# Two-layer encoder in split fp32: the last wide layer's second product in three sweeps over raw tiles, its weight sums made in the second attention

## The chip, the cores and the metric

The kernel is one launch on one core of a Trainium2 chip; input and output lie in the device's memory. The number is the device time in microseconds (us). Engines are named as in the profile: PE is TensorE (PEld its weight load), DVE is VectorE, ACT ScalarE, POOL GpSimd, SP SyncE, which here only issues DMAs.

## The reference

512 tokens of width 1024 pass two layers. Each layer adds an attention and then an MLP to the residual `h`, each on an RMS-normalised `h`. Layer 0 has a grouped-query and a latent attention side by side; layer 1 ("the second attention", C) has 16 heads of 64 in which each query sees a window of 8 x 16 grid neighbours, with a learned bias. A final RMSNorm ends it.

```python
def sq_relu_mlp(h, w_up, w_down):            # 1024 -> 4096 -> 1024
    u = jax.nn.relu(h @ w_up)
    return (u * u) @ w_down

for layer in range(2):
    hn = rmsnorm(h, norm_mix[layer])
    h = h + (hybrid_attention(hn, ...) if layer % 2 == 0
             else neighbourhood_attention(hn, od_w_qkv[i], od_rpb[i], od_w_out[i]))
    h = h + sq_relu_mlp(rmsnorm(h, norm_ffn[layer]), ffn_w_up[layer], ffn_w_down[layer])
return rmsnorm(h, final_norm)
```

All is fp32. The change lies in the MLP of layer 1 and in the second attention.

## The kernel before

**Products.** An fp32 operand is split in two parts, `hi` (a copy rounded by ScalarE) and `lo` (the difference, on VectorE); a product is three matmuls, hi x hi, hi x lo, lo x hi. Activations stand transposed: tile k holds 128 rows of the width and 512 columns, the tokens. The residual is `hT`, 8 such tiles; the MLP's hidden layer is 32 tiles. A *plain* product uses matmuls of 512 tokens (L501 to L503).

**Seven products.** `Seven` computes a 2 x 2 block product with seven block products instead of eight: the blocks are two k tiles ("a pair", kp) by two column groups of 128 in the weight, and two halves of 256 tokens. A matmul is then 256 wide (L388 to L390). The scheme needs sums of weight blocks, made by GpSimd in `seven_chunk` (L302 to L304; 256 KB of weight each, split at L308 and L309), and sums of token blocks, made by `Seven.sums` (L336, L338, L340, normally on GpSimd) and split by `Seven.split` (L362, L363).

**Weights.** `weights(i)` hands out chunk i of one list in order of use. SP loads five chunks ahead, the split is made two chunks ahead, and the split weights have three buffers. A `Slot` is a 256 KB buffer of a pool of 30.

**The second attention** (`attend_C`, some 640 to 815 us) works in 32 half-heads. `rest(w, us, ripe)` is called once in each: it fills TensorE with pieces of the q, k, v projection (`fill.run`), finishes an older head and normalises two blocks of softmax rows (`norm`: a reciprocal on VectorE, L1429, a multiplication on GpSimd, L1430), which TensorE then transposes (L1452). The order of instructions is written out by hand here (`fixed_order`), each engine's own. GpSimd's queue also moves q and k blocks there (L1338, L1358, L1359); SP loads weights and the bias.

**The MLP of layer 1** is `mlp(1, last)` with the sizes (6, 8, 6, 8, 4):

| from, us | to, us | stage | form |
|---|---|---|---|
| 837 | 869 | first product, 6 hidden tiles | plain |
| 869 | 898 | second product of these 6 | plain |
| 898 | 937 | first product, 8 tiles | seven |
| 937 | 981 | second product of these 8 | plain |
| 981 | 1070 | first product, 18 tiles: 6 split, 8 kept raw (fp32), 4 split | seven |
| 1070 | 1109 | second product of the 6; beside it `convert` makes the token sums of the 8 raw tiles, on VectorE | plain |
| 1109 | 1151 | second product of the 8, four groups m of 256 columns | seven |
| 1151 | 1184 | second product of the last 4 (`down`, two column halves c), norm, output | plain |

`hT` is turned back to token-major by 4 x 4 x 2 transposes (`turn(i, c)`, L1615 to L1619): those of c = 0 stand beside the seven-product second product (m 2 and 3), those of c = 1 in `down`.

Of the kernel before, what the change touches and what calls it, by code (L numbers as in the profile page):

```python
# [35 lines left out]
def encoder_kernel(ctx: ExitStack, tc: tile.TileContext, ins, out, dbg=None):  # L36
# [242 lines left out]
    def catch_up():  # L279
        take_up(off_d)  # L280
        take_up(off_a)
# [491 lines left out]
    rope_q(0)  # L773


    kst = Slot()

    def ev_kr(b):
# [331 lines left out]
    def first_product(l):  # L1110
# [7 lines left out]
        xp = [s_.pair() for s_ in X]  # L1118
        U, R = [], []
        rb = keep([P, S], F32, "rb")  # L1120
        state = dict(c=SIZES[l][0], ids=None, plain=False, split=iter(()))
        x7 = Seven(KD)

        def ev(j, b):
# [62 lines left out]
        def ahead():  # L1187
            state["ids"] = x7.plan(w, P * state["c"])

        def stage(n, raw=0, more=0):  # L1190

            if not state["plain"]:
                plain()
            left = n + raw + more - len(U)
            while left:
                i = state["ids"]
                state["c"] += 2
                left -= 2
                if left:
                    ahead()  # L1200
                for _ in x7.run(i, raw_evac if more <= left < more + raw else pair_evac):
# [13 lines left out]
    def bias_rows():  # L1215
        R, Fi, Fe = Slot(F32), Slot(F32), Slot(F32)
        rpb = ins["od_rpb"][0]
        for qr in range(8):
            SP.dma_start(R.t[16 * qr : 16 * qr + 16, 0:248],
                           rpb.rearrange("h a b -> h (a b)")[:, (7 - qr) * 31 : (7 - qr) * 31 + 248])  # L1220
            yield
        POOL.memset(Fi.t[:, 0:376], NEG)
        POOL.memset(Fe.t[:, 256:512], NEG)
        rv = R.t[:, 0:248].rearrange("p (k d) -> p d k", d=31)
        POOL.tensor_copy(Fi.t[:, 0:376].rearrange("p (j k) -> p j k", k=8)[:, 15:31, :], rv[:, 7:23, :])
        POOL.tensor_copy(Fe.t[:, 0:248].rearrange("p (j k) -> p j k", k=8), rv)
# [12 lines left out]
        for s_ in (R, Fi, Fe):  # L1239
            s_.free()  # L1240
        yield

    def convert(u7, R):
        held = tc.keep_in_program_order
# [167 lines left out]
    def attend_C(step):  # L1412
# [138 lines left out]
    def step(n):  # L1551
# [3 lines left out]
        if n == 12:  # L1555
# [3 lines left out]
            for x in rest:  # L1559
                fill.add(*x)  # L1560

    fill.run(LEAD)
    with fixed_order():
        fixed[0] = 1
        attend_C(step)
        give_low(len(ready))
        fixed[0] = 0
    ok = [s_.pair() for s_ in O[5:]]
# [8 lines left out]
    def last_mlp():  # L1577
# [43 lines left out]
        def down(k0, c, up, tail):  # L1621
# [5 lines left out]
            def run():  # L1627
                banks = group(4)

                def use(k, j):  # L1630
                    wh, wl = (x[:, k % 2, :] for x in weights(ids[k // 2]))
                    uh, ul = (up[k][:, z, j * P : (j + 1) * P] for z in range(2))
                    PE.matmul(banks[j], uh, wh, start=k == 0, stop=False)
                    PE.matmul(banks[j], uh, wl, start=False, stop=False)
                    PE.matmul(banks[j], ul, wh, start=False, stop=k == nk - 1)

                for k in range(nk - tail):
                    for j in range(4):
                        use(k, j)
                for j in range(4):  # L1640
                    for k in range(nk - tail, nk):
                        use(k, j)
                    if c == 0:
                        turn(j, 1)
                    add(j, c, banks[j])
                    (first_half, last_half)[c](j)
                    if c == 0 and j == 3:

                        ACT.activation(tiny(1), ones[:, 0:1], AF.Sqrt)
# [5 lines left out]
        def last(k0, tiles_):  # L1655
# [4 lines left out]
            def beside(m, i):  # L1660
                if m == 2 and i == 0:
# [67 lines left out]
```

## Time and profile before

| | us |
|---|---|
| three runs | 1183.44, 1183.66, 1183.66 (median 1183.66) |
| the profiled execution, its own time (span) | 1184.0 |
| TensorE busy in it | 1160.5 |
| VectorE, ScalarE, GpSimd busy | 883.2, 640.3, 526.1 |

The profiled execution is 0.3 us from the median. A window's row gives, for a stretch of the span, the time in which each engine was busy and its instructions, then the granted TensorE clock (1.00 is full), the mean busy share of the 16 DMA engines and the GB/s that they moved. A matmul's own duration (0.28 or 0.40 us) overlaps the next one's, so the cost of a matmul is the distance between starts. A row of a line's group gives operation, operands, shape and count, then busy us and mean ns of one, then the engine's idle time before it and what ended it.

### The profile page before, as it was taken

Reading aid. Unit: us, or ns where it says so; the run is one execution under the profiler, and the core shown is the slowest. Engines: PE = TensorE matmul, PEld = TensorE weight load, DVE = VectorE, ACT = ScalarE, POOL = GpSimd, SP = SyncE. Lnnn points to the kernel's source line nnn. Section 1 sums busy time; section 2 is a strip of 40 time slices with the busy share of each in tenths; the row PEclk is TensorE's granted clock in tenths of the full one; section 3 lists DMA queues with packets and bytes.
Section 4 is the critical chain, followed back from the end, with each engine's and each line's share of the span. In section 5 each row is a group of like instructions: output and inputs, shape, how many; then the busy total and the mean of one; then the engine's idle time right before and its main releaser. Section 6 shows DMA issues by size and latency. Waiting matters only on the chain.

```text
span 1184.0 us, 19784 instructions
## 1 busy us (share of the span) xinstructions
PE 1160.5 (98%) x7128; PEld 1021.2 (86%) x7128; DVE 883.2 (75%) x1514; ACT 640.3 (54%) x1081; POOL 526.1 (44%) x662
## 2 busy tenths in 40 slices
PE   9989999999999999999999999999999999999997
PEld 8667778888899899988998998988889989998895
DVE  5788998878967368786884676667996736778975
ACT  4468676664546247562553565555554624666344
POOL 3267343224562377819602232231376625774710
PEclk9999999999999999999999999999999999999998
DMA  7223225212524723225226464433352341322412
GB/s 244 71 54 92 68 78 134 62 56 77 167 86 134 263 70 90 72 90 165 67 72 178 131 184 126 116 112 109 107 165 76 115 134 55 98 64 89 143 36 71
DMA packets 110145, 128.01 MB, mean 108 GB/s; under 512 B 9075, under 2 KB 86816, under 8 KB 110048
## 3 DMA queue, kind: packets, MB, share of 16 engines
q1 hardware_dynamic: 106992, 119.30, 33.5%
q0 software_dynamic: 2304, 6.31, 2.2%
q8 instruction: 56, 0.92, 0.3%
q10 hardware_dynamic: 752, 1.15, 0.3%
q14 instruction: 41, 0.34, 0.1%
HBM read 104.32 MB, written 6.29 MB: 93 GB/s over the span
## 4 chain that ended last, share of the span: by engine, by line
PE 81%; DVE 4%; ACT 1%; issue 1%; POOL 0%; DVEq 0%; ACTq 0%
PE mm L503 8%; PE mm L501 8%; PE mm L502 8%; PE mm L390 4%; PE mm L389 4%; PE mm L388 4%; PE t L388 3%; PE t L389 3%; PE t L390 3%; PE s L502 2%; PE s L503 2%; PE s L501 2%; PE s L390 2%; PE s L388 2%; PE s L389 2%; PE s L997 2%
## 5 line engine op out<-in xcount | busy, mean ns | idle before, releaser
L309 DVE TENSOR_TENSOR wlo<-a,whi 128x896 fp32r<-128x896 f32 x132 | 161.8, 1230 | 83.7 <-ACT whi L308 82.9
L308 ACT ACTIVATE whi<-a 128x896 fp32r<-128x896 f32 x132 | 125.0, 950 | 155.0 <-PE o L502 45.8
L501 PE MATMUL mm<-a,whi 128*128 128x512 f32 x485 | 195.9, 406 | 0.9 <-DVE a L915 0.7
L503 PE MATMUL mm<-a,wlo 128*128 128x512 f32 x485 | 192.1, 397 | 2.5 <-DVE wlo L202 2.5
L502 PE MATMUL mm<-a,whi 128*128 128x512 f32 x485 | 192.5, 397 | 0.1
L202 DVE TENSOR_TENSOR wlo<-raw,whi 128x1024 fp32r<-128x1024 f32 (+4 forms) x117 | 139.3, 1193 | 66.4 <-ACT whi L212 63.9
L212 ACT ACTIVATE whi<-raw 128x1024 fp32r<-128x1024 f32 (+3 forms) x120 | 116.4, 971 | 92.2 <-PE s L502 39.8
L302 POOL TENSOR_TENSOR a<-a 128x128 f32<-128x128 f32 x132 | 85.1, 645 | 173.3 <-DMA a<-in_ffn_w_up_dram 103.9
L303 POOL TENSOR_TENSOR a<-a 128x256 f32<-128x256 f32 x132 | 120.2, 910 | 10.3
L304 POOL TENSOR_TENSOR a<-a 128x128 f32<-128x128 f32 x132 | 115.1, 872 | 10.3
L503 PEld LDWEIGHTS mm<-a,wlo 128*128 128x128 f32 x485 | 91.7, 189 | 23.7 <-DVE wlo L202 3.4
L501 PEld LDWEIGHTS mm<-a,whi 128*128 128x128 f32 x485 | 91.8, 189 | 20.4 <-PE t L972 0.9
L502 PEld LDWEIGHTS mm<-a,whi 128*128 128x128 f32 x485 | 91.9, 190 | 17.4 <-DVE a L545 0.4
L388 PE MATMUL mm<-a,whi 128*128 128x256 f32 x370 | 103.9, 281 | 0.0
L389 PE MATMUL mm<-a,whi 128*128 128x256 f32 x370 | 103.9, 281 | 0.0
L390 PE MATMUL mm<-a,wlo 128*128 128x256 f32 x370 | 103.7, 280 | 0.0
L1005 POOL TENSOR_SCALAR p<-p,ti 128x512 f32<-128x512 f32 x64 | 46.2, 724 | 92.3 <-DVE ti L1004 81.1
L1430 POOL TENSOR_SCALAR p<-p,ti 128x256 f32<-128x256 f32 x64 | 35.6, 567 | 104.8 <-DVE ti L1429 91.8
L388 PE MATMUL t<-a,whi 128*128 128x256 f32 x264 | 74.2, 281 | 0.0
L389 PE MATMUL t<-a,whi 128*128 128x256 f32 x264 | 74.1, 281 | 0.0
L390 PE MATMUL t<-a,wlo 128*128 128x256 f32 x264 | 73.9, 280 | 0.0
L390 PEld LDWEIGHTS mm<-a,wlo 128*128 128x128 f32 x370 | 69.6, 188 | 0.2 <-DVE wlo L309 0.2
(338 smaller groups left out, 3210.8 us busy)
## 6 DMA issues: line engine op xcount, KB each, us to landing
a<-in_ffn_w_up_dram SPq DMA_DIRECT2D x104, 256.0 KB
raw<-in_ffn_w_down_dram SPq DMA_DIRECT2D x46, 512.0 KB
raw<-in_od_w_qkv_dram SPq DMA_DIRECT2D x64, 128.0 KB
a<-in_ffn_w_down_dram SPq DMA_DIRECT2D x28, 256.0 KB
raw<-in_ffn_w_up_dram SPq DMA_DIRECT2D x12, 512.0 KB
raw<-in_ev_w_in_dram SPq DMA_DIRECT2D x12, 384.0 KB
a<-a SPq DMA_DIRECT2D x18, 256.0 KB
bias<-bx SPq DMA_DIRECT2D x16, 256.0 KB
```

Of the source, the lines that this page charges most:

```text
L202: z = lambda: (eng or DVE).tensor_tensor(to, src, f32(high), op=ALU.subtract)
L212: ACT.activation(hi[:, 0:m], raw[:, 0:m], AF.Copy)
L303: POOL.tensor_tensor(r[:, 4:6], r[:, 2:3].to_broadcast([P, 2, P]), r[:, 0:7:6], op=ALU.add)
L304: POOL.tensor_tensor(r[:, 7], r[:, 3], r[:, 5], op=ALU.subtract)
L308: ACT.activation(hi[:, 0:896], raw[:, 128:1024], AF.Copy)
L309: DVE.tensor_tensor(lo[:, 0:896], raw[:, 128:1024], f32(hi[:, 0:896]), op=ALU.subtract)
L388: PE.matmul(o, wh, x[:, 0], start=kp == 0 and n in (0, 1, 3, 5), stop=False, skip_group_check=True)
L389: PE.matmul(o, wh, x[:, 1], start=False, stop=False, skip_group_check=True)
L390: PE.matmul(o, wl, x[:, 0], start=False, stop=kp == self.np - 1, skip_group_check=True)
L501: PE.matmul(o, wh, xh, start=first, stop=False)
L502: PE.matmul(o, wh, xl, start=False, stop=False)
L503: PE.matmul(o, wl, xh, start=False, stop=last)
```

## The change

Layer 0's MLP is the same work (its code now takes the first size from `FIRST`). Layer 1's MLP becomes `mlp_swept`: 6 plain tiles and their plain second product as before, then the first product of all other 26 tiles in one stretch (13 groups, 52 weight chunks, instead of 8 + 18 tiles with a plain product between); 22 of the tiles stay raw, the last 4 go to `down` as before. The second product of the 22 tiles (11 pairs) is a seven-product in another arrangement, `Sweeps`: the seven block products are dealt to three passes over all 11 pairs, two products in passes 0 and 1, three in pass 2, for all 1024 columns at a time, and each pass adds its banks straight into `hT`. `convert` and the plain second products of 8 and 6 tiles are gone.

The token blocks are made pair by pair by `tokens`, a step ahead: differences on GpSimd, splits on ScalarE and VectorE. The weight blocks are made by `SumsAhead` during the second attention, one step in each of `rest` 1 to 22: per pair four sums on GpSimd and two loads and two stores of 512 KB on GpSimd's queue, into a device buffer `made`. SP then loads the blocks from the weight (pass 0) or `made` (passes 1 and 2). The 16 transposes `turn(j, 0)` and their 4 copies move into `down` for c = 0, between its main part and its tail.

```diff
+    class SumsAhead:
+        def load(self, kp):
+            ...
+                for z, s_ in enumerate(self.raw[kp]):
+                    POOL.dma_start(s_.t, self.w[k * P : (k + 1) * P, :])
+        def steps(self):
+            self.load(0)
+            self.load(1)
+            yield
+            for kp in range(self.n):
+                ...
+                POOL.tensor_tensor(a22, a21, a22, op=ALU.add)
+                POOL.tensor_tensor(a21, a11, a21, op=ALU.subtract)
+                if kp:
+                    self.load(kp + 1)
+                yield
+                POOL.tensor_tensor(a11, a22, a11, op=ALU.subtract)
+                POOL.tensor_tensor(a12, a12, a11, op=ALU.subtract)
+                for z, s_ in enumerate(two):
+                    POOL.dma_start(self.made[kp, z], s_.t)
+                    s_.free()
+                yield
...
+    def sweep_chunk(w, k0, kind, made):
+        ...
+        if kind == 0:
+            for z in range(2):
+                SP.dma_start(line(a[:, S * z : S * z + S]), half(k0 + z, 0))
+        else:
+            for z in range(2):
+                SP.dma_start(line(a[:, S * z : S * z + S]), blocks(made[z])[:, (z, 1 - z)[kind - 1]])
+        if kind == 2:
+            SP.dma_start(line(b[:, 0:S]), half(k0 + 1, 1))
+        yield
+        ...
+        ACT.activation(hi, a, AF.Copy)
+        DVE.tensor_tensor(lo, a, f32(hi), op=ALU.subtract)
+        if kind == 2:
+            third = Slot()
+            ACT.activation(third.t[:, 0:S], b[:, 0:S], AF.Copy)
+            DVE.tensor_tensor(third.t[:, S:], b[:, 0:S], f32(third.t[:, 0:S]), op=ALU.subtract)
...
+    class Sweeps:
+        def tokens(self, kind, kp):
+            ...
+            if kind == 0:
+                split_to(d[:, :, 0], d[:, :, 1], r[:, 0:4:2])
+                POOL.tensor_tensor(r[:, 0:2], r[:, 1:4:2], r[:, 0:2], op=ALU.subtract)
+                if kp < 2:
+                    self.two(kp)
+            elif kind == 1:
+                for q, src in enumerate((r[:, 0], s2)):
+                    split_to(d[:, q, 0], d[:, q, 1], src)
+                if kp + 2 < self.n:
+                    self.two(kp + 2)
+                if kp + 3 >= self.n:
+                    self.four(kp + 3 - self.n)
+            else:
+                if kp + 3 < self.n:
+                    self.four(kp + 3)
+                ...
+                split_to(d[:, :, 0], d[:, :, 1], r[:, 1:3])
+                split_to(e[:, 0], e[:, 1], r[:, 3])
+        def run(self, R):
+            ...
+            for i, (kind, kp) in enumerate(steps):
+                if i + 1 < len(steps):
+                    ready_[steps[i + 1]] = self.tokens(*steps[i + 1])
+                w_ = weights(self.ids[kind][kp])[0]
+                ...
+                for q, w_, x, n in todo:
+                    for m in range(4):
+                        mm(kind, n, m, w_, x, q == 0 and (kind, n) in starts, q == self.n - 1)
+                        yield kind, kp
...
+    def mlp_swept(l, made, last=None):
+        ...
+        R, V = stage(0, RAW[l], MORE[l], lambda: sweeps.append(Sweeps(w, FIRST, made)))[1:]
+        reserve[0] = 6
+        for kind, kp in sweeps[0].run(R):
+            beside(kind, kp)
...
             for x in w:
                 norm(*x)
+            next(sums1, None)
             catch_up()
...
+                if c == 0:
+                    for j in range(4):
+                        turn(j, 0)
                 for j in range(4):
                     for k in range(nk - tail, nk):
                         use(k, j)
...
-                if m > 1 and i in (16, 22):
-                    turn(2 * (m - 2) + (i == 22), 0)
...
-        mlp(1, last)
+        mlp_swept(1, ahead1, last)
+        flip[0] = 1
```

Line numbers of the kernel after: the two normalisations are L1683, the sums L805, L806, L810 and L811, their loads L796 and stores L813; in the sweeps the weight's low half is L1309, a token's L1349, the matmuls L1401 to L1403 and the adds L1407.

GpSimd in the second attention, early. Before, only normalisations and moves of q and k stand there:

```order
L1430 TENSOR_SCALAR p_7106<-p_7106,ti_7111 128x256
L1430 TENSOR_SCALAR p_7106<-p_7106,ti_7113 128x256
L1430 TENSOR_SCALAR p_7151<-p_7151,ti_7156 128x256
L1430 TENSOR_SCALAR p_7151<-p_7151,ti_7158 128x256
L1338 DMA a_7174<-a_7173 64x1024 x2
L1358 DMA a_7198<-a_7198 64x512
L1359 DMA a_7198<-sc_7199 64x512
L1430 TENSOR_SCALAR p_7220<-p_7220,ti_7225 128x256
```

The same place after:

```order
L1683 TENSOR_SCALAR p_7117<-p_7117,ti_7122 128x256
L1683 TENSOR_SCALAR p_7117<-p_7117,ti_7124 128x256
L810 TENSOR_TENSOR a_6944<-a_6945,a_6944 128x2x256
L811 TENSOR_TENSOR a_6945<-a_6945,a_6944 128x2x256
L813 DMA made_6943<-a_6944 128x1024
L813 DMA made_6943<-a_6945 128x1024
L1683 TENSOR_SCALAR p_7166<-p_7166,ti_7171 128x256
L1683 TENSOR_SCALAR p_7166<-p_7166,ti_7173 128x256
L805 TENSOR_TENSOR a_6949<-a_6948,a_6949 128x2x256
L806 TENSOR_TENSOR a_6948<-a_6948 128x2x256
L796 DMA a_7206<-in_ffn_w_down_dram 128x1024
L796 DMA a_7207<-in_ffn_w_down_dram 128x1024
```

Between two pairs of normalisations now stand two sums and, in nearly every gap, two loads or two stores.

VectorE beside the plain second product of the 6, before; `a_12008` and `a_11983` are token sums and splits of `convert`, `wlo_12030` a low half that TensorE needs next:

```order
L1265 TENSOR_TENSOR hT<-hT,t_11849 128x512
L338 TENSOR_TENSOR a_12008<-a_11591,a_12008 128x256
L1265 TENSOR_TENSOR hT<-hT,o_11850 128x512
L340 TENSOR_TENSOR a_12008<-a_11591,a_12008 128x256
L202 TENSOR_TENSOR wlo_12030<-raw_11861,whi_12029 128x1024
L363 TENSOR_TENSOR a_11983<-a_11591,a_11983 128x256
```

After, where pass 0 ends and pass 1 begins:

```order
L1349 TENSOR_TENSOR a_12163<-a_11683,a_12163 128x256
L1407 TENSOR_TENSOR hT<-hT,t_11686 128x2x256
L1309 TENSOR_TENSOR wlo_12058<-a_11947,whi_12057 128x1024
L1407 TENSOR_TENSOR hT<-hT,t_11687 128x2x256
L1407 TENSOR_TENSOR hT<-hT,s_11688 128x2x256
L1407 TENSOR_TENSOR hT<-hT,o_11689 128x2x256
L1309 TENSOR_TENSOR wlo_12099<-a_11982,whi_12098 128x1024
```

The token sums have left VectorE (they stand on GpSimd), and between two low halves of weights stand three adds into `hT`.

More of the change, by code (lines that the diff above doesn't have):

```diff
@@ L1120, in first_product @@
         rb = keep([P, S], F32, "rb")
-        state = dict(c=SIZES[l][0], ids=None, plain=False, split=iter(()))
+        state = dict(c=FIRST, ids=None, plain=False, split=iter(()))
         x7 = Seven(KD)
@@ L1188, in ahead, with stage @@
             state["ids"] = x7.plan(w, P * state["c"])
-        def stage(n, raw=0, more=0):
+        def stage(n, raw=0, more=0, then=lambda: None):
             if not state["plain"]:
@@ new lines, in mlp_swept, with ev @@
+    def mlp_swept(l, made, last=None):
+        stage, ahead, later = first_product(l)
+        w = ins["ffn_w_down"][l]
+        bias = bias_rows() if l == 0 else iter(())
+        U = stage(FIRST)[0]
+        up = [s_.pair() for s_ in U]
+        def ev(m, b):
+            DVE.tensor_tensor(hT[:, m, :], hT[:, m, :], b, op=ALU.add)
+        gens = [product(w, 0, up, tiles(512 * c, 512), lambda j, b, c=c: ev(4 * c + j, b)) for c in range(2)]
+        ahead()
+        for c, gen in enumerate(gens):
+            for i, _ in enumerate(gen):
+                later(c, i)
+        for s_ in U:
+            s_.free()
+        reserve[0] = 3
+        sweeps = []
+        R, V = stage(0, RAW[l], MORE[l], lambda: sweeps.append(Sweeps(w, FIRST, made)))[1:]
+        reserve[0] = 6
+        beside = last(FIRST + RAW[l], V) if last else lambda kind, kp: next(bias, None)
+        for kind, kp in sweeps[0].run(R):
+            beside(kind, kp)
+        for _ in bias:
+            pass
+        reserve[0] = 1
@@ L1560, in step @@
                 fill.add(*x)
+    ahead1 = SumsAhead(ins["ffn_w_down"][1], FIRST, RAW[1] // 2)
+    sums1 = ahead1.steps()
+    next(sums1)
     fill.run(LEAD)
@@ L1565, in encoder_kernel @@
         attend_C(step)
+        assert next(sums1, 0) == 0 and not ahead1.raw
         give_low(len(ready))
@@ L1658, in last, with beside @@
             runs.extend(down(k0, c, up, 2 + 2 * c) for c in range(2))
-            def beside(m, i):
-                if m == 2 and i == 0:
+            def beside(kind, kp):
+                if (kind, kp) == (2, 6) and not H:
                     H.extend(Slot(F32) for _ in range(4))
```

132 lines of the change are left out of this document (added).

## The prediction

> **What bounds the kernel now.** I read the page's busy line and its chain first, then the windows that cut the last half into stages, then the one long TensorE wait in the stretch that the change rewrites, and last the prices on GpSimd, which gets new work. A change of 0.2% (2.4 us) is about the least that a measurement of this kernel tells from no change.
>
> ```profile
> span 1184.0 us, 19784 instructions
> PE 1160.5 (98%) x7128; PEld 1021.2 (86%) x7128; DVE 883.2 (75%) x1514; ACT 640.3 (54%) x1081; POOL 526.1 (44%) x662
> PE 81%; DVE 4%; ACT 1%; issue 1%; POOL 0%; DVEq 0%; ACTq 0%
> ```
>
> TensorE is busy 98% of the span and holds 81% of the chain: matmul time counts almost one for one, and every wait of TensorE too. The windows give each stage's rate:
>
> ```profile
> core 0: us, PE busy (x) PEld busy (x) DVE busy (x) ACT busy (x) POOL busy (x), PEclk, DMA share, GB/s
> 640.00:755.00 115.00, 114.84 (x751) 103.95 (x750) 76.29 (x216) 66.70 (x158) 34.90 (x67) 1.00 0.56 150
> 940.00:978.00 38.00, 38.00 (x166) 30.80 (x165) 15.51 (x18) 10.27 (x11) 12.17 (x18) 1.00 0.44 141
> 985.00:1065.00 80.00, 80.00 (x680) 80.00 (x679) 61.89 (x70) 50.03 (x62) 58.26 (x72) 1.00 0.28 80
> 1099.00:1107.00 8.00, 5.77 (x18) 4.31 (x17) 8.00 (x10) 1.93 (x3) 7.05 (x9) 0.79 0.55 171
> 405.00:415.00 10.00, 10.00 (x45) 8.10 (x44) 2.33 (x2) 0.99 (x2) 5.63 (x9) 1.00 0.98 343
> ```
>
> A seven-product stage (985 to 1065) runs 679 weight loads, one for each 256-wide matmul, in 80.00 us: 0.1178 us each. A plain stage (940 to 978) runs 165 in 38.00: 0.2303 us for a 512-wide one. Only 1099 to 1107 falls short, with VectorE full (8.00 of 8) and the granted clock at 0.79:
>
> ```profile
> 1099.95 0.40 PE L502 MATMUL mm<-a,whi 128*128 128x512 f32 x1
> 1102.58 0.79 PE L503 MATMUL mm<-a,wlo 128*128 128x512 f32 x1 [2.23 <-DVE wlo L202]
> 1105.73 0.52 PE L501 MATMUL mm<-a,whi 128*128 128x512 f32 x1
> 1106.09 0.40 PE L502 MATMUL mm<-a,whi 128*128 128x512 f32 x1
> ```
> ```profile
> 1100.24 0.89 DVE L340 TENSOR_TENSOR a<-a,a 128x256 f32<-128x256 f32 x1
> 1101.05 1.47 DVE L202 TENSOR_TENSOR wlo<-raw,whi 128x1024 fp32r<-128x1024 f32 x1
> ```
>
> The matmul at 1102.58 should start 0.23 after 1099.95, at 1100.18: it is 2.40 late, because the low half of its weight (L202) stood on VectorE behind token sums and adds. Eight starts later the trace is at 1106.09: 3.51 us for 8 steps that take 1.84 at full rate, another 1.67 at a lowered clock. The stall costs 2.40 + 1.67 = 4.07 us.
>
> **The matmuls.** In the second MLP, 14 of the hidden tiles leave the plain second product: 14 x 8 x 3 = 336 matmuls of 512 fewer. The seven-product second product grows from 8 tiles to 22, 4 pairs to 11: 7 pairs x 4 x 7 x 3 = 588 of 256 more. Nothing else on TensorE changes in number. -336 x 0.2303 + 588 x 0.1178 = -77.4 + 69.3 = **-8.1 us**. Here nothing has to be guessed, as both rates are held for whole stages.
>
> **The stall.** `convert` goes, and its plain stage: **-4.1 us**. Late next could be VectorE in the sweeps, so I price a step there:
>
> ```profile
> L202 DVE TENSOR_TENSOR wlo<-raw,whi 128x1024 fp32r<-128x1024 f32 x88 | 113.2, 1288 | 55.7 <-ACT whi L212 53.4 <-PE o L390 2.2
> L202 DVE TENSOR_TENSOR wlo<-raw,whi 128x512 fp32r<-128x512 f32 x6 | 4.7, 780 | 1.3 <-ACT whi L212 1.3
> L363 DVE TENSOR_TENSOR a<-a,a 128x512 fp32r<-128x512 f32 x51 | 41.2, 846 | 0.7 <-ACT a L362 0.7
> L363 DVE TENSOR_TENSOR a<-a,a 128x256 fp32r<-128x256 f32 x17 | 9.7, 573 | 0.0
> ```
>
> A step of sweep 0 is 24 matmuls, 2.83 us, with 1.29 + 0.85 = 2.14 us of VectorE; of sweep 1, 2.83 with 1.29 + 2 x 0.57 = 2.43; of sweep 2, 36 matmuls, 4.24, with 1.29 + 0.78 + 0.85 + 0.57 = 3.49. All fit, at 76 to 86%. At the end of sweeps 0 and 1 four adds of 128x512 come on top (`L1265` of them is among the rows that held up the low half above), but weights lead by two splits, the restarted banks are used late, and the order puts one split between the adds: **0**, at worst the stall's 4.1 once more. The sweeps' loads are 512 KB in 2.83 us and 768 KB in 4.24, 185 GB/s; the window from 405 to 415 moved 343. GpSimd's token differences there replace three sums for each of 16 weight chunks and `convert`'s:
>
> ```profile
> L336 POOL TENSOR_TENSOR a<-a 128x512 f32<-128x512 f32 x8 | 14.1, 1763 | 43.1 <-DVE a L1142 43.1
> L338 POOL TENSOR_TENSOR a<-a,a 128x256 f32<-128x256 f32 x8 | 9.4, 1174 | 0.6
> ```
>
> At these prices, the dearest in the trace, a step of sweep 0 needs 1.76, and of sweeps 1 and 2 mostly 1.17, at most 2.35, within 2.83 and 4.24: **0**, unless VectorE falls behind first.
>
> **Sums of the weights in the second attention.** This is the dear part. Between 640 and 805 us TensorE runs 128 score matmuls in 32 half-heads, 5.35 us each, and each ends in two normalisations on GpSimd (L1430; L1683 afterwards) for which transposes wait:
>
> ```profile
> L1426 PE MATMUL s<-a,a x128: 275/280/288, 639.5 to 805.3; 128*128 128x256 f32 x128
> ```
> ```profile
> 716.49 0.94 POOL L1430 TENSOR_SCALAR p<-p,ti 128x256 f32<-128x256 f32 x2 [6.19 <-DVE ti L1429]
> 721.66 0.94 POOL L1430 TENSOR_SCALAR p<-p,ti 128x256 f32<-128x256 f32 x2 [4.23 <-DVE ti L1429]
> ```
> ```profile
> 718.45 0.60 PE L1452 MATMUL t<-cst,p 128*128 128x128 f32 x4
> 723.52 0.60 PE L1452 MATMUL t<-cst,p 128*128 128x128 f32 x4
> ```
>
> The pairs come 5.17 us apart, and the transposes start some 1.0 us after a pair ends: GpSimd has the gap between pairs, and little more, to do something else. Into 22 gaps go two sums of 128x2x256 each and on average two DMA issues, loads and stores, all ahead of the next pair on an engine that works in order. These rows bound the price:
>
> ```profile
> L202 POOL TENSOR_TENSOR wlo<-raw,whi 128x512 fp32r<-128x512 f32 x10 | 14.5, 1451 | 5.2 <-ACT whi L222 4.1 <-ACT whi L212 1.1
> L595 POOL TENSOR_TENSOR sc<-sc,sc 128x512 fp32r<-128x512 f32 x5 | 6.4, 1290 | 22.1 <-DVE sc L594 22.1
> L1338 POOL DMA_DIRECT2D a<-a x16 | 8.7, 544 | 61.5 <-DVE a L830 56.2 <-ACT p L1460 4.2 <-PE s L1426 1.1
> ```
>
> Free time: 22 half-heads are 117.7 us, of which GpSimd is idle (115.00 - 34.90) / 115.00, or 82.0 us. Needed: 44 issues x 0.545 = 24.0 us, and 44 sums x t. At t = 1.29 (L595, beside a waiting VectorE) that is 80.8 and fits: 0. At 1.451 (L202 on GpSimd, the same 512 elements beside a busy VectorE) it is 87.8: 5.8 over. At 1.763 (L336, in `convert`, VectorE full) it is 101.6: 19.6 over. VectorE is 66% busy in this attention, so I take the middle row: **+5.8 us**. A gain is excluded, since nothing is taken off GpSimd or TensorE there.
>
> That GpSimd's price depends on VectorE shows in the long up stage, where one form at one place takes 0.46 and 1.31 us:
>
> ```profile
> 1015.47 0.46 POOL L302 TENSOR_TENSOR a<-a 128x128 f32<-128x128 f32 x1 [4.54 <-DMA a<-in_ffn_w_up_dram]
> 1025.67 1.31 POOL L302 TENSOR_TENSOR a<-a 128x128 f32<-128x128 f32 x1
> 1057.73 0.47 POOL L302 TENSOR_TENSOR a<-a 128x128 f32<-128x128 f32 x1
> ```
>
> The Trainium skill, "SBUF — State Buffer", section "Who interferes with whom", has the reason: a VectorE instruction with two SBUF inputs and a GpSimd instruction that reads SBUF exclude each other for a whole instruction. By that rule a sum that always meets such an instruction would cost as at L336, and the forecast would be 13.8 us higher; the trace has both durations, and the attention meets it only at times.
>
> **One up stage of 26 tiles.** Its GpSimd sums are the slowest supplier. From the first row above (chunk 19) to the last (chunk 35) 16 chunks took 42.26 us, 2.64 each; TensorE uses one in 21 x 0.1178 = 2.47. It falls back by 0.17 a chunk, 52 x 0.17 = 8.6 us at most over the stage. The lead:
>
> ```profile
> 1029.78 0.28 PE L388 MATMUL mm<-a,whi 128*128 128x256 f32 x1
> 1069.49 0.28 PE L388 MATMUL mm<-a,whi 128*128 128x256 f32 x1
> ```
>
> These are where TensorE begins with chunks 19 and 35: 14.3 us after GpSimd's first sum of the one, 11.8 after the other. From those 11.8 some 3 us go off for a chunk's sums and two splits, so 36 chunks leave about 9; the 16 more would eat 2.7 of them: **0**, at worst 8.6.
>
> **Turned columns.** The 16 transposes `turn(j, 0)` move from the seven-product down to the last plain one, with four copies on ScalarE, which idles there:
>
> ```profile
> 1156.64 1.06 ACT L212 ACTIVATE whi<-raw 128x1024 fp32r<-128x1024 f32 x1 [4.64 <-PE o L1635]
> ```
>
> No count changes: **0**, a few tenths either way.
>
> **The sum.** The durations are of one execution of 1184.0 us, 0.3 above the median of 1183.66 (1183.44 to 1183.66). 1184.0 - 8.1 - 4.1 + 5.8 = 1177.6; less 0.3, **1177.3 us**.
>
> **Rivals.**
> (a) GpSimd's free time is enough, t near 1.29: 1177.3 - 5.8 = 1171.5. For it: a step is issued right behind a pair, when the gap begins. Against: VectorE runs 66% there.
> (b) The other side: GpSimd becomes the bound of the second attention. Every pair of normalisations stands behind a step, the transposes wait for the pair, and the rest of the head behind them. It decides from t = 1.6, where 44 x 1.6 + 24.0 - 82.0 = 12.4 takes back the 12.2 gained. At L336's 1.763 the time is 1177.3 + 13.8 = 1191.1.
> (c) The DMA engines fill up. 44 x 512 KB is 23.07 MB; at the 343 GB/s that a share of 0.98 moved (405 to 415) that is 67.3 us at 0.98, a share of 0.56 over 117.7 us, on top of the 0.56 there. 1.12 is 14 us too much, if nothing can slide later. GpSimd would wait for its own loads, with the normalisations behind them. 1171.5 + 14 = 1185.5; with half of it absorbed, 1178.5. Against: SP's loads run ahead there and can slide. The Trainium skill, "DMA: Bandwidth & Descriptors", section "Issuing engines are not separate DMA queues", speaks for this case: issuing from GpSimd adds no bandwidth, all share the 16 engines; no run here shows two queues full at once.
> (d) The long up stage is supplied too slowly, or VectorE's stall comes back in a sweep: 1177.3 + 4.1 to + 8.6, 1181.4 to 1185.9.
>
> **How the numbers follow.** Forecast 0.49, (a) 0.15, (b) 0.18, (c) 0.10, (d) 0.08. Against 1183.66 the bounds of 0.2% are 1181.3 and 1186.0. The forecast's own spread, t from 1.35 to 1.55, is 1172.9 to 1181.7: 0.46 of it faster, 0.03 the same. (a) is faster. (b) reaches from 1183.9 to 1191.1: the same for 0.04, slower for 0.14. (c) is faster for 0.03, the same for 0.03, slower for 0.04; (d) the same for 0.06, slower for 0.02. Faster 0.64, same 0.16, slower 0.20. The range cuts the upper part of (b) and the lower tail of (a): 1170.5 to 1188; the forecast's own is 1173 to 1182.
>
> **What would show it.** Right: the sweeps' windows full of matmuls at 0.1178 us each, no wait for a low half above 1 us, and the second attention some 6 us longer than the 165.8 between the first and last score above, with TensorE waiting there for GpSimd's normalisations and sums at 1.4 to 1.5 us. Wrong: sums at 1.3 or 1.7, GpSimd waiting for the raw weights, TensorE waiting for low halves late in the up stage, or a clock below 1 in a sweep.

## The result and the profile after

The changed kernel takes 1204.3 us (median of 4 runs, 1203.24 to 1205.6) against 1183.66: 1.017 of the time before, interval 1.0155 to 1.0184. Slower by 20.6 us, where 1177.3 was forecast and 1188 was the range's end. The profiled execution has a span of 1202.9. First its page: span, engines, chain of work, and the software queue, which carries GpSimd's moves.

```profile
span 1202.9 us, 20568 instructions
PE 1158.3 (96%) x7380; PEld 1032.1 (86%) x7380; DVE 897.5 (75%) x1521; ACT 656.8 (55%) x1116; POOL 618.5 (51%) x735
PE 74%; DVE 4%; DMA 4%; POOL 2%; issue 2%; ACT 2%; SPq 0%; DVEq 0%; POOLq 0%; ACTq 0%
q0 software_dynamic: 8640, 29.38, 7.7%
```

TensorE's share of the chain fell from 81% to 74%, and DMA, which was not in it, holds 4%, GpSimd 2%. TensorE is even busy 2 us less in all; what grew is its waiting. The windows say where: the second attention, and the first two passes of the sweeps.

```profile
core 0: us, PE busy (x) PEld busy (x) DVE busy (x) ACT busy (x) POOL busy (x), PEclk, DMA share, GB/s
640.00:760.00 120.00, 106.48 (x659) 94.81 (x658) 70.27 (x187) 58.27 (x139) 102.44 (x129) 0.97 0.91 275
1060.00:1080.00 20.00, 16.33 (x117) 15.98 (x116) 18.27 (x15) 6.93 (x11) 19.77 (x17) 0.83 0.43 137
1080.00:1100.00 20.00, 16.28 (x121) 15.67 (x120) 18.98 (x24) 10.33 (x21) 14.15 (x12) 0.91 0.39 122
1110.00:1140.00 30.00, 30.00 (x256) 30.00 (x255) 24.25 (x34) 20.74 (x31) 0.00 (x0) 1.00 0.79 254
```

In the attention TensorE stood still 13.5 of 120 us, with the DMA share at 0.91 and GpSimd busy 102 of 120. In passes 0 and 1 (here from 1060 to 1100 us) it lost 7.4 of 40 us, and the granted clock fell to 0.83 and 0.91. From 1110 to 1140 (the end of pass 1 and a part of pass 2), with GpSimd idle, nothing is lost, though DMA moves 254 GB/s. TensorE's waits, longest totals first (line waited at, releaser, us in total, times, longest):

```profile
PE s L1679 <- DMA a<-sc: 9.6, 2, 7.2
PE t L1705 <- POOL p L1683: 6.4, 4, 2.5
PE t L1403 <- DVE wlo L1309: 4.3, 3, 3.7
PE mm L1403 <- DVE wlo L1309: 3.4, 2, 2.4
```

The first two are the attention (scores wait for a move of q, transposes for a normalisation), the last two the sweeps (low halves of weights). They come to 16.0 and 7.7 us; most of what the landmarks below show beyond that is matmuls at a lowered clock behind the longest of these waits (last section).

By landmarks, before against after: from the first score to the first one of the last half-head 165.4 and 186.4 us, so **+21.0** ("scores over", from here on). The 924 matmuls of the sweeps start over 122.4 us where 108.7 are due at 0.1178 each: **+13.7**. The long up stage starts its 1092 matmuls in 128.8 us, 0.1180 each: a loss of 0.3 us at most. Profiled executions also differ by up to 2.5 us in the first 95 us of the span, with the same code there (the first score stood at 639.5 before and 637.0 after), so stages are compared from their own starts.

The moves in the attention. These are DMA issues of the same kind, of before for the whole span and of after between 640 and 760 us (count, KB each, median us from issue to landing):

```profile
a<-a POOLq DMA_DIRECT2D x16, 256.0 KB, 3.4
a<-sc POOLq DMA_DIRECT2D x8, 128.0 KB, 3.7
```
```profile
a<-a POOLq DMA_DIRECT2D x8, 256.0 KB, 9.2
a<-sc POOLq DMA_DIRECT2D x5, 128.0 KB, 7.3
```

The q and k moves land in 7 to 9 us where they took 3.4 to 3.7. Behind them stands another one, on SP's queue, that waits for them; the worst case, in the timelines of SP's queue and TensorE:

```profile
699.15 0.47 SPq L1616 DMA_DIRECT2D a<-sc  x1
```
```profile
710.95 0.58 PE L1679 MATMUL s<-a,a 128*128 128x256 f32 x1 [7.17 <-DMA a<-sc]
```

128 KB issued at 699.15 release the scores at 710.95, 11.8 us later. The sums themselves had the price that was forecast:

```profile
L806 POOL TENSOR_TENSOR a<-a 128x512 f32<-128x512 f32 x11 | 17.5, 1590 | 0.9
L811 POOL TENSOR_TENSOR a<-a,a 128x512 f32<-128x512 f32 x11 | 15.9, 1445 | 0.9
L805 POOL TENSOR_TENSOR a<-a,a 128x512 f32<-128x512 f32 x11 | 15.4, 1403 | 1.9 <-DMA a<-in_ffn_w_down_dram 1.9
L810 POOL TENSOR_TENSOR a<-a,a 128x512 f32<-128x512 f32 x11 | 14.1, 1283 | 0.0
```

1.43 us on average; the forecast took 1.451.

The sweeps. VectorE, GpSimd and TensorE around the longest wait in pass 0:

```profile
1060.56 2.36 DVE L871 TENSOR_TENSOR a<-a,a 128x512 fp32r<-128x512 f32 x2
1062.85 3.96 DVE L1309 TENSOR_TENSOR wlo<-a,whi 128x1024 fp32r<-128x1024 f32 x2
```
```profile
1060.05 1.18 POOL L1339 TENSOR_TENSOR a<-a,a 128x256 f32<-128x256 f32 x1
1061.19 1.18 POOL L1335 TENSOR_TENSOR a<-a 128x256 f32<-128x256 f32 x1
1062.45 1.05 POOL L1339 TENSOR_TENSOR a<-a,a 128x256 f32<-128x256 f32 x1
1063.47 2.25 POOL L1354 TENSOR_TENSOR a<-a 128x512 f32<-128x512 f32 x1
```
```profile
1064.65 0.58 PE L1403 MATMUL t<-a,wlo 128*128 128x256 f32 x1 [3.67 <-DVE wlo L1309]
1065.02 0.41 PE L1401 MATMUL t<-a,whi 128*128 128x256 f32 x1
1065.24 0.41 PE L1402 MATMUL t<-a,whi 128*128 128x256 f32 x1
```

VectorE and GpSimd both work without a gap, and a low half takes 2.0 us. L1335 and L1339, the short differences that passes 1 and 2 need, run in the middle of pass 0: the code writes most of them one a step in the later passes, but they are ready early, and the scheduler put them ahead.

### The profile page after: what moved, and what is told of

Its sections match the earlier page's. It is cut to its first block, busy times and chain, and to the rows that moved or that the text cites. A ratio compares the mean times of both kernels' runs of the same rounds, so it can differ in the third digit from the quotient of the medians.

```text
span 1202.9 us, 20568 instructions
## 1 busy us (share of the span) xinstructions
PE 1158.3 (96%) x7380; PEld 1032.1 (86%) x7380; DVE 897.5 (75%) x1521; ACT 656.8 (55%) x1116; POOL 618.5 (51%) x735
## 4 chain that ended last, share of the span: by engine, by line
PE 74%; DVE 4%; DMA 4%; POOL 2%; issue 2%; ACT 2%; SPq 0%; DVEq 0%; POOLq 0%; ACTq 0%
PE mm L501 6%; PE mm L503 6%; PE mm L502 6%; PE mm L390 3%; PE mm L389 3%; PE mm L388 3%; PE t L389 2%; PE t L388 2%; PE t L390 2%; PE s L502 2%; PE s L503 2%; PE s L501 2%; PE s L390 2%; PE s L388 2%; PE s L389 2%
## 5 line engine op out<-in xcount | busy, mean ns | idle before, releaser
L309 DVE TENSOR_TENSOR wlo<-a,whi 128x896 fp32r<-128x896 f32 x116 | 142.1, 1227 | 70.3 <-ACT whi L308 69.7
L308 ACT ACTIVATE whi<-a 128x896 fp32r<-128x896 f32 x116 | 109.8, 949 | 128.4 <-PE o L502 36.6
L501 PE MATMUL mm<-a,whi 128*128 128x512 f32 x443 | 178.5, 405 | 1.0 <-DVE a L956 0.7
L502 PE MATMUL mm<-a,whi 128*128 128x512 f32 x443 | 174.9, 395 | 0.1
L503 PE MATMUL mm<-a,wlo 128*128 128x512 f32 x443 | 174.3, 394 | 0.3 <-DVE wlo L202 0.3
L202 DVE TENSOR_TENSOR wlo<-raw,whi 128x1024 fp32r<-128x1024 f32 (+4 forms) x103 | 122.7, 1195 | 48.6 <-ACT whi L212 48.4
L302 POOL TENSOR_TENSOR a<-a 128x128 f32<-128x128 f32 x116 | 73.8, 636 | 99.9 <-DMA a<-in_ffn_w_up_dram 67.8
L503 PEld LDWEIGHTS mm<-a,wlo 128*128 128x128 f32 x443 | 83.1, 188 | 19.0 <-DVE wlo L202 0.8
L501 PEld LDWEIGHTS mm<-a,whi 128*128 128x128 f32 x443 | 83.5, 189 | 18.4 <-PE t L1013 0.8
L304 POOL TENSOR_TENSOR a<-a 128x128 f32<-128x128 f32 x116 | 94.5, 815 | 9.1
L502 PEld LDWEIGHTS mm<-a,whi 128*128 128x128 f32 x443 | 83.5, 189 | 15.4 <-DVE a L545 0.4
L389 PE MATMUL mm<-a,whi 128*128 128x256 f32 x330 | 92.7, 281 | 0.0
L388 PE MATMUL mm<-a,whi 128*128 128x256 f32 x330 | 92.5, 280 | 0.0
L389 PE MATMUL t<-a,whi 128*128 128x256 f32 x232 | 65.2, 281 | 0.0
L388 PE MATMUL t<-a,whi 128*128 128x256 f32 x232 | 65.0, 280 | 0.0
L390 PEld LDWEIGHTS mm<-a,wlo 128*128 128x128 f32 x330 | 62.1, 188 | 0.2 <-DVE wlo L309 0.2
L389 PEld LDWEIGHTS mm<-a,whi 128*128 128x128 f32 x330 | 62.0, 188 | 0.1
```

The costliest lines, as they stand in the source:

```text
L202: z = lambda: (eng or DVE).tensor_tensor(to, src, f32(high), op=ALU.subtract)
L304: POOL.tensor_tensor(r[:, 7], r[:, 3], r[:, 5], op=ALU.subtract)
L308: ACT.activation(hi[:, 0:896], raw[:, 128:1024], AF.Copy)
L309: DVE.tensor_tensor(lo[:, 0:896], raw[:, 128:1024], f32(hi[:, 0:896]), op=ALU.subtract)
L388: PE.matmul(o, wh, x[:, 0], start=kp == 0 and n in (0, 1, 3, 5), stop=False, skip_group_check=True)
L389: PE.matmul(o, wh, x[:, 1], start=False, stop=False, skip_group_check=True)
```

## The experiments

Theory A: the attention lost its time to the bytes moved. Rival A': to GpSimd's sums ahead of the normalisations. Theory B: the sweeps lost theirs because GpSimd's differences stretch VectorE's splits. Rival B': VectorE has too much to do by itself. Each was tried by leaving one part out; where weight sums or token differences are left out, passes and splits read the plain blocks in the same shapes.

**Nothing ahead.**

```diff
-            next(sums1, None)
...
-        mlp_swept(1, ahead1, last)
+        mlp_swept(1, RawMade(ins["ffn_w_down"][1], FIRST, RAW[1] // 2), last)
```

> Leaves out the weight sums of the second attention with their loads and stores; passes 1 and 2 load the raw weight blocks in the same shapes instead. Every theory of the attention's loss: the attention is back at the 176.4 us of before (197.4 in the changed kernel), so 1204.3 - 21.0 = 1183.3 us, with the 13 us that the sweeps lose still in it. If it stays above 1190, part of the loss is not from this work.

Measured 1184.74 us, 1.0008 of before (0.9999 to 1.0017); scores over 165.5 us, sweeps still 122.4. All of the attention's loss comes from this work, and the sweeps' loss has nothing to do with it.

**Sums alone, moves alone.**

```diff
-                if kp:
-                    self.load(kp + 1)
...
-                for z, s_ in enumerate(two):
-                    POOL.dma_start(self.made[kp, z], s_.t)
```

> Keeps the 44 sums on GpSimd at their places but leaves out all loads and stores after the first four (sums go over the same two pairs again; passes 1 and 2 load raw blocks). Theory 'moves' (the attention lost its time to DMA engines that were full, q and k copies landing late): the sums at 1.43 us fit GpSimd's free 82.0 us, so 1183 to 1186 us. Theory 'GpSimd' (normalisations late behind the sums): 1195 us or more.

```diff
-                POOL.tensor_tensor(a22, a21, a22, op=ALU.add)
-                POOL.tensor_tensor(a21, a11, a21, op=ALU.subtract)
...
-                POOL.tensor_tensor(a11, a22, a11, op=ALU.subtract)
-                POOL.tensor_tensor(a12, a12, a11, op=ALU.subtract)
```

> Keeps the loads and stores on GpSimd's queue and leaves out the 44 sums. Theory 'moves': most of the 21 us stays, 1197 to 1203 us, with the DMA share still over 0.9. Theory 'GpSimd': 1184 to 1188 us, since GpSimd has then only 24 us of issues more.

Sums alone: 1184.27 us, scores over 166.5, 1.1 more than before. Moves alone: 1198.16 us, scores over 178.2, 12.8 more. The windows of the two from 640 to 760 us, sums alone first:

```profile
640.00:760.00 120.00, 119.22 (x784) 107.80 (x783) 85.37 (x224) 68.78 (x164) 96.50 (x112) 1.00 0.54 145
```
```profile
640.00:760.00 120.00, 110.72 (x685) 99.37 (x684) 71.78 (x207) 63.07 (x149) 53.69 (x103) 0.96 0.94 296
```

GpSimd busy 96.50 of 120 leaves TensorE at 119.22; a DMA share of 0.94 takes 9 us from it. A' is out as a cause by itself. Both together cost 21.0, 7.1 more than the two apart. ScalarE's waits in the changed kernel from 636 to 826 us show a part of how the moves and sums add up:

```profile
ACT a L874 <- DMA made<-a: 14.0, 3, 7.1
```

A step frees its two buffers as soon as it has issued their stores. ScalarE's next k block (L874) is written into such a buffer and waits until the store has landed, 14.0 us in three waits, and ScalarE's exponentials and splits stand behind it in order. With the moves alone these waits came to 4.4 us, and with half of the bytes (below) there were none. Buffers that are not reused at once were not tried, so how much of the 7.1 us this is stays open.

**Bytes or instructions.** The moves alone, but half the columns.

```diff
-                    POOL.dma_start(s_.t, self.w[k * P : (k + 1) * P, :])
+                    POOL.dma_start(s_.t[:, 0:S], self.w[k * P : (k + 1) * P, 0:S])
...
-                    POOL.dma_start(self.made[kp, z], s_.t)
+                    POOL.dma_start(self.made[kp, z][:, 0:S], s_.t[:, 0:S])
```

> As the kernel with the moves alone (no sums, 1198.2 us), but each load and store moves half of its columns: the same 44 instructions on GpSimd's queue, 11.5 MB instead of 23.07 (passes 1 and 2 load raw blocks). Theory 'bytes': 0.28 more of the DMA share on top of 0.56 is 0.84, and nearly nothing of the attention's 12 to 13 us stays: 1185 to 1188 us. Theory 'instructions' (GpSimd's queue, its order and the latency of issues): 1195 us or more.

1185.14 us, scores over 165.5. The same instructions, at a share of 0.79, cost nothing:

```profile
640.00:760.00 120.00, 119.84 (x791) 108.86 (x790) 80.72 (x225) 69.56 (x165) 56.36 (x107) 1.00 0.79 232
```

It is the bytes, and what waits for them to land, not the number of instructions. **Spread over 32 half-heads** instead of 22, with everything else as changed:

> The 22 steps of sums and moves are spread over all 32 half-heads instead of the first 22. Theory 'moves': 23.07 MB over 171 us instead of 118 adds a DMA share of 0.38 instead of 0.56; 0.94 in the first 115 us is at the limit and well below it later, so half or more of the 21 us comes back: 1190 to 1196 us. If it were only the moves' place in GpSimd's order, the same number of steps would cost the same: 1202 or more.

1194.45 us, scores over 176.7: about half of the attention's loss is back. The share alone does not tell where the rest is lost. The first 100 us and a short stretch of this kernel, then a short stretch of the half moves (same columns):

```profile
637.00:737.00 100.00, 98.25 (x623) 87.84 (x623) 67.57 (x183) 56.26 (x134) 74.58 (x102) 1.00 0.84 247
740.00:748.00 8.00, 5.15 (x36) 4.52 (x34) 5.15 (x14) 4.36 (x9) 3.70 (x6) 1.00 1.00 340
```
```profile
690.00:700.00 10.00, 10.00 (x71) 9.26 (x70) 7.71 (x21) 6.10 (x15) 4.65 (x9) 1.00 1.02 310
```

In the 100 us at 0.84 TensorE stood still for 1.75 us. Its longest wait, 3.2 us for a normalisation, ends at 748.4, behind 8 us at 1.00; but the half moves had 10 us at 1.02 and lost nothing there (a transfer counts whole in the stretch in which it starts, so a share can pass 1). How long the moves take to land orders the kernels better. The 256 KB moves of k from 640 to 760 us landed, at the median, in 3.8 us with the sums alone, 5.0 with half moves, 6.8 here, 6.9 with the moves alone and 9.2 in the changed kernel; the scores took 1.1, 0.1, 11.3, 12.8 and 21.0 us longer than before.

**No token differences.** The 33 of GpSimd beside the sweeps are left out.

```diff
-            POOL.tensor_tensor(s2, r[:, 3], r[:, 0], op=ALU.subtract)
...
-            POOL.tensor_tensor(r[:, 2], s2, r[:, 2], op=ALU.subtract)
...
-                POOL.tensor_tensor(r[:, 0:2], r[:, 1:4:2], r[:, 0:2], op=ALU.subtract)
```

> Leaves out the 33 differences of token blocks on GpSimd beside the sweeps (the splits read the unsummed blocks, in the same number and shape). Theory 'port' (VectorE's splits take 1.7 to 2.3 us beside GpSimd's differences and 1.21 without, so TensorE waits for low halves): the sweeps run full, 1204.3 - 12 = 1192 us. Theory 'VectorE has too much work of its own': 1201 us or more.

1191.99 us; the sweeps take 109.3 us of the 108.7 due. B' is out: VectorE does its own work in time.

**When GpSimd works.** All three differences held in the written order (first edit); then also the two short ones paced, by a dependency on the VectorE split issued before them (second edit):

```diff
-            POOL.tensor_tensor(s2, r[:, 3], r[:, 0], op=ALU.subtract)
+            tc.keep_in_program_order(POOL.tensor_tensor(s2, r[:, 3], r[:, 0], op=ALU.subtract))
...
```
```diff
+            if self.lo_ is not None:
+                tc.add_manual_dep(z.ins, self.lo_.ins.name, ...
...
+            self.pace(POOL.tensor_tensor(s2, r[:, 3], r[:, 0], op=ALU.subtract))
...
```

> The same 33 token differences on GpSimd, but held to the order in which they are written (the changed kernel's scheduler puts most of the 22 short ones, which are needed only in passes 1 and 2, into pass 0). If it matters when GpSimd works beside VectorE: pass 0 has 13 of them instead of some 25 and loses less, while the rest, ready at once, run as a burst in pass 1; the sweeps' loss of 13 us goes to 6 to 10, 1197 to 1201 us. If only the number matters: 1204.

> As the held kernel, and each short difference also waits for the VectorE split of its own step, so that there is about one GpSimd difference in each of the 33 steps. Theory 'port': VectorE's split of a weight is stretched from 1.2 to about 2.0 us once a step, and passes 0 and 1 have 0.8 to 1.0 us to spare, so the loss goes to 2 to 5 us: 1193 to 1196 us. If pacing changes nothing, 1198 or more, pass 0's own 11 long differences are enough for the loss.

1201.7 and 1199.27 us; the sweeps lose 10.1 and 7.9 us instead of 13.7. The place in the order explains 3.6 to 5.8 us; the rest stays although the differences come about one a step. The held kernel lies just above its range. The paced one was expected at 1193 to 1196 if the differences' place were nearly all of it, a miss: what a difference takes from VectorE was put too low.

**The differences on VectorE.**

```diff
-            POOL.tensor_tensor(s2, r[:, 3], r[:, 0], op=ALU.subtract)
+            DVE.tensor_tensor(s2, r[:, 3], r[:, 0], op=ALU.subtract)
...
```

The other two differences are moved in the same way.

> The 33 differences go to VectorE itself (0.68 us for 128x512, 0.42 for 128x256, about 17 us in all; GpSimd idle in the sweeps). Theory 'port': VectorE's work in the sweeps is then 76 + 9.5 + 17 = 102 us of 109 without stretching, so the loss falls to 0 to 3 us: 1191 to 1194 us. Theory 'VectorE has too much work of its own': the loss grows, 1206 us or more.

1193.39 us, sweeps over 109.7. VectorE's groups in the first 54 us of the sweeps (pass 0 and a part of pass 1), of the changed kernel (1046 to 1100 us) and of this one (1047 to 1101):

```profile
L1309 DVE TENSOR_TENSOR wlo<-a,whi 128x1024 fp32r<-128x1024 f32 x12 | 18.8, 1573 | 0.5 <-ACT whi L1308 0.4
L1349 DVE TENSOR_TENSOR a<-a,a 128x512 fp32r<-128x512 f32 x9 | 9.8, 1110 | 0.7 <-ACT a L1348 0.7
```
```profile
L1309 DVE TENSOR_TENSOR wlo<-a,whi 128x1024 fp32r<-128x1024 f32 x15 | 18.2, 1219 | 0.3 <-ACT whi L1308 0.3
L1349 DVE TENSOR_TENSOR a<-a,a 128x512 fp32r<-128x512 f32 x9 | 6.0, 683 | 0.0
L1354 DVE TENSOR_TENSOR a<-a 128x512 f32<-128x512 f32 x9 | 6.1, 683 | 0.0
```

A low half takes 1.22 us instead of 1.57, a token's split 0.68 instead of 1.11, and the long difference on VectorE 0.68. On GpSimd it takes 1.28 us at its shortest. A step of pass 0 has one low half and one such split, so GpSimd's work beside them stretched them by 0.35 + 0.43 = 0.78 us on average, more than the 0.68 that the long difference takes on VectorE: the engine that was to be relieved is better off doing the work.

**Neither cause.** Differences on VectorE, nothing ahead:

> Both causes gone: the token differences on VectorE, and no weight sums or moves at all (passes 1 and 2 load raw blocks). What is left is the rearranged second product and the lost stall. If the forecast's two gains are right (8.1 us of matmuls, 4.1 us of stall): 1171.5 to 1173 us. If the stall is worth little in runs without a profile: 1175 to 1177.

1173.59 us, 0.9911 of before (0.9898 to 0.9924): the rearranged second product, with the stall gone, is worth 10.6 us (9 to 12). It lies between the two expected ranges.

**Complete kernels that keep it.** All have the differences on VectorE; they differ in where the 11 pairs of weight sums are made. The edit for 3 pairs right after the first attention and 8 in the second:

```diff
+        if n == 58:
+            next(early)
...
     attend(all_heads(), step)
+    next(early, None)
...
-            next(sums1, None)
+            if 16 * turns1[0] // 32 > 16 * (turns1[0] - 1) // 32:
+                next(sums1, None)
```

The first hunk loads two pairs late in the first attention; the steps then follow among the parts of its output projection.

> Two edits together: token differences on VectorE (1204.3 to 1193.4 alone) and steps over 32 half-heads (1204.3 to 1194.5 alone). They lie in different stages, so if the gains add: 1183.5 us.

> Token differences on VectorE, and the weight sums with their moves in three places: 3 pairs beside the first attention, 2 before the second, 6 over its 32 half-heads (a DMA share of 0.21 more there instead of 0.56). If both causes are gone, what is left is the change's gain in matmuls and the stall, 8.1 + 4.1 us: 1172 to 1176 us, faster than both. If the first attention pays for what it takes on: 1178 or more.

> Complete kernel: token differences on VectorE; the weight sums of 2 pairs right after the first attention, held there in GpSimd's order, 2 pairs before the second attention, 7 over its 32 half-heads. The first version in three places lost about 8 us in the first attention, where 3 pairs' sums stood close together; if that was their place, this one is at 1174 to 1178 us, faster than both. If any sums ahead of the second attention cost what they save there: 1183.

> As the last, but with no pair beside the first layer: 2 pairs before the second attention, 9 over its 32 half-heads, where the DMA share rises by 0.32. By the half moves (0.28 more cost under 2 us) the attention loses 1 to 4 us: 1174 to 1178 us.

> Complete kernel: token differences on VectorE; weight sums of 4 pairs right after the first attention, none just before the second (where 2 pairs made VectorE late by some 8 us), 7 pairs over its 32 half-heads. From the kernel with neither (1173.6): 1.5 to 4 us for the 4 early pairs, 2 for the attention: 1177 to 1180 us, faster than both. If GpSimd is then late with the next layer's token sums: 1182 or more.

> As the last with 3 pairs early and 8 in the second attention: 1 to 3 us for the early ones, 2 to 4 for the attention: 1177 to 1180 us.

> As the last with 2 pairs early and 9 in the second attention: 1.5 us for the early ones (one wait of 1.25 us in the trace of the version with 2 early and 2 before), 4 to 6 for the attention: 1179 to 1182 us.

| pairs: in or right after the first attention, before the second, in its 32 half-heads | us | of before | scores over, us |
|---|---|---|---|
| 0, 0, 11 | 1184.73 | 1.0001 (0.999 to 1.0012) | 176.3 |
| 3 in it, 2, 6 | 1185.18 | 1.0015 (1.0003 to 1.0027) | 166.5 |
| 2 after, 2, 7 | 1187.22 | 1.0035 (1.0022 to 1.0047) | 167.4 |
| 0, 2, 9 | 1186.51 | 1.0024 (1.001 to 1.0037) | 170.2 |
| 4 after, 0, 7 | 1180.89 | 0.9973 (0.9964 to 0.9982) | 167.4 |
| 3 after, 0, 8 | 1176.99 | 0.9944 (0.9931 to 0.9956) | 166.8 |
| 2 after, 0, 9 | 1177.29 | 0.9947 (0.9935 to 0.9959) | 166.4 |

Three of my four first guesses missed. The first added as foreseen. The next three took the load off the second attention, as their scores show, and paid for it at the new place: beside the first attention TensorE waited 5.3 us for VectorE in one piece, and just before the second attention VectorE's normalisation was late (the version with 2 after and 2 before, its waits from 600 to 640 us, where before has none):

```profile
PE t L530 <- DVE r L1578: 4.3, 1, 4.3
PE o L1653 <- DVE a L508: 2.1, 2, 1.1
PE t L522 <- DVE acc L517: 1.6, 1, 1.6
```

Why VectorE was late there was not taken apart. The count of pairs alone does not decide in the attention either: with 9 pairs in it the scores took 170.2 us in one kernel and 166.4 in another, each in its one profiled execution. Of the last three guesses, 4 pairs came 0.9 us above its range, 3 pairs at the lower end of its own, and 2 pairs 1.7 us below.

With nothing just before the second attention and 3 pairs right after the first, held in GpSimd's order, the kernel is faster than both: 1176.99 us. Its second attention (first row) has the share at 0.76, and 1060 to 1100 us (second row: passes 0 and 1, and the start of pass 2) run full on a VectorE that is busy 39 of 40 us:

```profile
640.00:760.00 120.00, 119.88 (x781) 108.48 (x780) 80.65 (x223) 67.60 (x160) 72.99 (x108) 1.00 0.76 224
1060.00:1100.00 40.00, 39.69 (x339) 39.49 (x338) 39.01 (x71) 25.86 (x43) 0.00 (x0) 1.00 0.66 204
```

**The stall by itself.** The kernel before, with the last pair's token sums on GpSimd:

```diff
-            yield from u7.sums(kp, raw, DVE, held)
+            yield from u7.sums(kp, raw, DVE if kp < 3 else POOL, held)
```

> The kernel before with the token sums of the last of its four raw pairs on GpSimd instead of VectorE, so that three instructions of about 2.1 us are gone ahead of the late low half. If the stall is worth what was read from its rows (2.4 us of wait and 1.7 at a lower clock): 1179.6 to 1181 us. If it only moves to another low half: 1183 to 1185.

1183.78 us, 0.9997 (0.9988 to 1.0006): no gain. Its trace has the distance between starts at 2.05 us instead of 2.63, and no lowered clock behind it; from the start of the first seven-product stage to the last matmul it is 1.7 us shorter, of the 4.1, and the timed runs show none of it. Inconclusive: it shrank the wait and did not remove it, and a lowered clock behind such a wait is not in every execution (last section).

## Why the prediction was wrong, by its steps

- **The matmuls and the stall, -12.2 us: about right.** The kernel with neither cause is 10.6 us faster than before, and its sweeps are 1.2 us over what 0.1178 us a matmul gives. How much of it is the stall was not settled.
- **The second attention, +5.8: this term is +21.0.** The step that failed is the sum of "free time" and "needed", which counted a move as 0.545 us of issue on GpSimd and as nothing else. The sums' price was right (1.43 for 1.451), and sums alone cost 1.1. The bytes stood in the prediction only as rival (c), at a chance of 0.10, although its own sum came to a share of 1.12. It was discounted by "SP's loads run ahead there and can slide"; what could not slide were the short q and k moves, chained over two queues, which landed in 7 to 9 us instead of 3.4 to 3.7, and ScalarE's writes into buffers whose stores had not landed. And (c) was priced as the whole loss, up to 14, where the moves alone cost 12.8 and with the sums 21.0. The Trainium skill, "DMA: Bandwidth & Descriptors", section "Issuing engines are not separate DMA queues", said that another queue gives no more bandwidth; the share of 0.94 with the moves alone agrees.
- **The sweeps, 0, "at worst the stall's 4.1 once more": this term is +13.7.** The step that failed is "All fit, at 76 to 86%" and, for GpSimd, "within 2.83 and 4.24": two engines were each set against the step's time alone. Undisturbed, a step of pass 0 has 1.22 + 0.68 = 1.90 us on VectorE and 1.28 on GpSimd; if they cannot overlap that is 3.18 of 2.83 us, before any short difference is added. The port was used in the prediction to price GpSimd, and not to price VectorE beside it. The Trainium skill, "SBUF — State Buffer", section "Who interferes with whom", says that a VectorE instruction with two SBUF inputs contends with a GpSimd instruction that reads SBUF, and calls the port an exclusive lock; the trace agrees that both get longer (a low half 1.57 us with GpSimd beside it, 1.22 without; a long difference up to 2.25 on GpSimd, 1.28 at its shortest). Whether they exclude each other wholly no run here shows. The differences' place was to be read from GpSimd's order in the sweeps, where I had looked at VectorE's alone.
- **One up stage, 0: right** (0.1180 us a matmul to its end). **Turned columns, 0: no loss seen**: from the last sweep's end to the last matmul it is 2.0 us longer, with the 16 transposes that came from the stage ahead; what they took there was not measured by itself.

What came was (b)'s sign by (c)'s mechanism, plus (d)'s late low halves in a sweep at three times the 4.1 us. Both errors have one form: a resource that two engines share was counted once for each.

## What to carry to other kernels

Price moved work on every resource it uses, the bytes on the DMA engines and the port between VectorE and GpSimd among them, and add what is there already; at a mean share of 0.79 nothing was lost here with half of each move, and short stretches above 1 did no harm either; the loss came where the short moves on which scores wait took 6.8 us and more to land instead of 5.0. Look also at who is handed a buffer whose store has not landed. Before giving VectorE's work to GpSimd, add both engines' undisturbed times: here the sum, 3.18 us, was over the step's 2.83, and VectorE was slower for the help. Work that may be done any time belongs where its own resource is idle, and it must be held there, since a scheduler puts early what is ready early.

## What the runs showed of the hardware

The granted clock fell to half behind waits that were shorter than I had thought: distances between starts of 2.63 us (before), 2.69 and 3.95 us (after) were each followed by 3 to 5 us of matmuls at nearly twice their distance (0.43 us for 0.23, and 0.21 for 0.1178), while 2.05 us (the stall's kernel) and 1.22 us (after) were not. The length alone does not decide. At the same place early in the span (74.6 and 73.6 us) before and after have a distance of 2.78 and 2.77 us; these are the windows just behind it, before first:

```profile
75.00:78.50 3.50, 3.50 (x10) 2.73 (x9) 2.39 (x8) 2.74 (x8) 0.69 (x1) 0.53 0.00 0
```
```profile
74.00:77.50 3.50, 3.50 (x18) 2.67 (x17) 3.23 (x12) 2.67 (x8) 0.75 (x2) 1.00 0.00 0
```

The clock is 0.53 behind the one and 1.00 behind the other, with the same code, and this is a part of the 2.5 us by which executions differ early. In the sweeps a distance of 2.16 us was followed by 0.50 in the paced kernel and by 1.00 in the held one:

```profile
1075.20:1078.60 3.40, 3.40 (x18) 3.40 (x18) 3.15 (x3) 1.47 (x3) 3.40 (x3) 0.50 0.01 2
```
```profile
1074.30:1077.00 2.70, 2.70 (x23) 2.70 (x24) 2.23 (x2) 1.68 (x3) 2.70 (x3) 1.00 0.01 3
```

So the price of a wait of this length is itself uncertain: 3.4 us at half clock cost 1.7 us, as in the stall, or nothing. The Trainium skill, "TensorE: Matmul & The Clock Gate", section "Part 1: The HAM clock gate", states an idle window of about 3.4 us for it; here distances of 2.2 to 2.8 us were enough in some places and not in others.
